# A feed-forward stage on one core: f as three 256-column products a tile, its relu taken from PSUM by ScalarE, and squares and forms issued last in a step

## The chip, the cores and the metric

The kernel runs on one NeuronCore of a Trainium2 chip. The engines named below are TensorE (PE, with its weight loads as PEld), VectorE (DVE), ScalarE (ACT), GpSimd (POOL) and SyncE (SP, which issues DMAs). The metric is the device time of one execution in microseconds (us). Before the change three runs gave 1714.46, 1715.00 and 1715.11 us, median 1715.0; the execution that was profiled took 1715.43 us, of which the span from the first to the last instruction is 1713.6 us.

## The reference, cut to what matters

One encoder block on x of 256 tokens and 2048 channels: a gated linear attention branch and a Hyena branch, merged, projected, normalized, and then the feed-forward part, which is all that the change touches:

```python
h = _layernorm(DEEPNORM_ALPHA * h + mix, ln1_g[l], ln1_b[l])
ff = jnp.square(jax.nn.relu(h @ w_ff1[l])) @ w_ff2[l]
h = _layernorm(DEEPNORM_ALPHA * h + ff, ln2_g[l], ln2_b[l])
```

`w_ff1` is 2048 x 8192 and `w_ff2` is 8192 x 2048, all float32.

## The kernel before, in words

**Precision.** Every float32 operand is split into a high part (a cast by ScalarE, `CAST hi<-src`) and a low part (VectorE subtracts the high part from the source, `TENSOR_TENSOR lo<-src,hi`). A product a·b becomes three TensorE products: high·high, high·low, low·high, summed in PSUM. So each weight block costs ScalarE one pass, VectorE one pass and TensorE three products.

**f, the first matrix.** `hT` holds the normalized input, transposed, as `hT[:, kt, part, token]` for 16 blocks `kt` of 128 channels, part 0 high and part 1 low. One tile of f is 128 feed-forward channels by 256 tokens, summed over the 16 blocks. Before the change `channel_products` makes it in one PSUM tile of 512 columns, in two halves `[:, 0]` and `[:, 1]`: per block one product of 512 columns with the high weights against high and low activations side by side (line 197, `f<-hT,whi`), and one of 256 columns with the low weights against the high activations, added to the first half (line 201, `f<-hT,wlo`). `quad_sum` then brings the two halves together: ScalarE copies the second half to `low` (`COPY f_l<-f`) and VectorE adds the first half to it, into the f tile of a pair in SBUF (`TENSOR_TENSOR dfth_fr<-f,f_l`, or `dftl_fr` or `sum_fr`: five buffers that pairs n = 0 to 31 use in turn). Two tiles (c = 0 and 1) make a pair n; `squares(n)` runs relu and then square over the pair on ScalarE (lines 1252 and 1253).

**The second matrix.** For most of `w_ff2` it is done by pairs of tiles, in Strassen-like form with seven products w0 to w6 instead of eight. `forms(n)` builds the stationary operands of a pair: three small VectorE sums (`fw`), two ScalarE casts and two VectorE subtractions into a slot of `fa`. The weights of a step arrive in a ring tile, from which `plain_split` (`b_h`, `b_l`, the two `ring` additions and two accumulating DMAs that POOL issues), `pair_split` (`whi`, `wlo` from `ring`) and `last_split` (two pieces at the end of `fa`) make the pieces. `form_products` issues three products of 512 columns for each w.

**The step.** `ff_pairs` runs 56 joint steps s = 0 to 55. Step s makes one tile of f for a later pair (n, c = divmod(s + 8, 2)) and the seven products of one pair of the second matrix. TensorE gets, in the order of the program: w0 to w2 and w3, w4 of step s, then f (both weight halves), then w5 and w6 of the step before. Meanwhile ScalarE and VectorE split what step s + 1 needs: `plain_split`, `half_split(s + 1, 0)` (the first half of f's weights, `whi`, `wlo` from `fraw`), `pair_split`, then in even steps `squares`, in the 27 steps that the table FORMED lists (5, 6, 8, 9, 10, 14, 15, 17, 19, 20 and so on) `forms`, then `quad_sum` of this step's f, then `half_split(s + 1, 1)` and `last_split`. w0 to w6 are seven PSUM banks that are summed over a run of steps (seven runs, RUNS); at a run's end `take_sums` drains them. w2, w3 and w4 hold three of the four banks of the pool that f uses, so f has one bank: the next tile of f cannot begin before this one has been drained.

**The order.** Inside `ff_pairs` the ScalarE and VectorE work, and the first and third product of each w, are pinned to the order of the program (`pin`); a scheduler places the rest, among it the products of f. Each engine runs its instructions in the order given. An engine that waits for one instruction holds up all that stand behind it.

Of the kernel before, what the change touches and what calls it, by code (L numbers as in the profile page):

```python
# [12 lines left out]
AF = mybir.ActivationFunctionType  # L13
# [3 lines left out]
P = 128  # L17
D = 2048
L = 256
NT = L // P  # L20
KT = D // P
# [10 lines left out]
LEAD = 8  # L32
# [3 lines left out]
FORMED = dict(zip((5, 6, 8, 9, 10, 14, 15, 17, 19, 20, 24, 25, 27, 29, 30, 34, 35, 37, 39, 40, 44, 45, 47, 49, 50, 53, 54,  # L36
                   SLOTS + 1), range(LEAD // 2, D_FF // P // 2)))
# [12 lines left out]
def block_kernel(  # L50
# [25 lines left out]
    nc = tc.nc  # L76
    MM = nc.tensor.matmul
# [19 lines left out]
    def psum_main(name):  # L97
        return mmp.tile([P, 512], F32, tag="mm", name=name)
# [83 lines left out]
    def channel_psum(name):  # L182
        return psum_main(name).rearrange("p (a b) -> p a b", a=2)

    def in_turn(w):
        return w.rearrange("p (a b) -> p b a", a=2)

    def both_in_turn(t):
        return t.rearrange("p k (a b) -> p k b a", a=2)

    def channel_products(ps, act, half, kts, plain=False):
        hi, lo = half
        at = [(kt, slice(kt % 8 * P, (kt % 8 + 1) * P)) for kt in kts]

        def high():
            for kt, js in at:
                MM(ps, hi[:, js], act[:, kt] if plain else both_in_turn(act[:, kt]), start=(kt == 0), stop=(kt == KT - 1))  # L197

        def low():
            for kt, js in at:  # L200
                MM(ps[:, 0], lo[:, js], act[:, kt, 0] if plain else in_turn(act[:, kt, 0]), start=False, stop=False)  # L201

        for part in (high, low) if kts[0] == 0 else (low, high):
            part()

    def channel_sum(dst, ps, name, scale=1.0):
        low = base.tile([P, L], F32, tag="low", name=name)
        with tc.high_priority():
            nc.scalar.activation(low, ps[:, 1], AF.Copy, scale=scale)
            nc.vector.scalar_tensor_tensor(dst, ps[:, 0], scale, low, op0=ALU.mult, op1=ALU.add)  # L210
# [67 lines left out]
    def act_tile(pool, tag, name):  # L278
        return pool.tile([P, KT, 2, L], F32R, tag=tag, name=name)
# [14 lines left out]
    with tc.tile_pool(name="xp", bufs=1) as xp, tc.tile_pool(name="xq", bufs=1) as xq:  # L294
# [25 lines left out]
        for i in range(3):  # L320
            t = weight_half(-1, i, True)
# [17 lines left out]
        for k0, n in PIECES:  # L339
            raw = pieces[k0]  # L340
            kts = range(k0, k0 + n)
            split_hi_lo(xT[:, k0:k0 + n, 0], xT[:, k0:k0 + n, 1], raw[:, :, 0:L])
            w = raw[:, :, L:].rearrange("p k (b j) -> p k b j", b=OPENING)
# [9 lines left out]
            if k0 == 0:  # L353
                hi, lo = places[0]
# [162 lines left out]
    for i in range(2 * NCH):  # L517
        c, o = divmod(i, 2)
        n = 4 + (i * 21) // 15
# [597 lines left out]
    hT = act_tile(ep, "hT", "hT")  # L1117
# [107 lines left out]
    def quads(n):  # L1225
        return quad_tiles[n % 5]
# [3 lines left out]
    def pin(ins):  # L1230
        return tc.keep_in_program_order(ins) if pinned[0] else ins

    def VT(dst, a, b, op):
        return pin(nc.vector.tensor_tensor(dst, a, b, op=op))  # L1234

    def cast(hi, src):
        return pin(nc.scalar.copy(hi, src))  # L1237
# [4 lines left out]
    def quad_sum(i, c, ps, name, plain=False):  # L1242
        low = base.tile([P, L], F32, tag="low", name=name)
        dst = quads(i)[:, 2 * c:2 * c + 2][:, ::-1]
        halves = [a.rearrange("p (t j) -> p t j" if plain else "p (j t) -> p t j", j=P) for a in (ps[:, 0], low)]
        with tc.high_priority():
            cast(low, ps[:, 1])
            return VT(dst, halves[0], halves[1], ALU.add)

    def squares(n):  # L1250
        q = quads(n)
        pin(nc.scalar.activation(q, q, AF.Relu))
        return pin(nc.scalar.activation(q, q, AF.Square))


    def forms(n):
        q, slot, plain = quads(n), fa_slot(n % 8), n >= SLOTS // 2
        hi, lo = slot[:, 0], slot[:, 1]
        if plain:
            cast(hi[:, 0:4], q)  # L1260
            rest(lo[:, 0:4], q, hi[:, 0:4])
            return
        t = ep.tile([P, 3, P], F32, tag="ft", name=f"fw{n}")
        VT(t[:, 0:2], q[:, 0:1].broadcast_to([P, 2, P]), q[:, 1:3][:, ::-1], ALU.subtract)
        VT(q[:, 0], q[:, 1], t[:, 0], ALU.subtract)
        VT(t[:, 2], q[:, 3], q[:, 0], ALU.subtract)
        for part, c in ((q, slice(0, 4)), (t, slice(4, 7))):
            cast(hi[:, c], part)
            rest(lo[:, c], part, hi[:, c])
# [45 lines left out]
    def last_split(p):  # L1315
        fa_slot(4)
        hi, lo = (t[:, 7168:8192] for t in fa)
        split_units(p, 2, hi, lo, raw_units(p)[:, 1:3])
# [8 lines left out]
    half_parts = {}  # L1327
# [53 lines left out]
    def take_sums(pss, p, ks):  # L1381
        if 0 <= p < SLOTS:
            begin, end, g, pair = run_of(p)
            if p == end - 1:
                for k in ks:
                    take_sum(pair == 0, g, k, pss[k])
# [30 lines left out]
    def ff_pairs():  # L1417
        pss = [psum_side(f"w{j}") if j not in (2, 3, 4) else psum_main(f"w{j}") for j in range(7)]
        joins = []
        for s in range(SLOTS):  # L1420
            more = s + 1 < SLOTS
            n, c = divmod(s + LEAD, 2)
            pinned[0] = True
            form_products(pss, s, 0, (0, 1, 2))
            form_products(pss, s, 1, (3, 4))
            ps = channel_psum(f"f{n}_{c}")
            for h in range(2):
                channel_products(ps, hT, half_parts.pop((s, h)), range(8 * h, 8 * h + 8))
            if s:
                form_products(pss, s - 1, 2, (5, 6))  # L1430
            if s + 2 < SLOTS:
                ring_load(s + 2)
            if more:
                plain_split(s + 1)
                half_split(s + 1, 0)
            take_sums(pss, s, (0, 1, 2))
            if more:
                pair_split(s + 1)
            take_sums(pss, s, (3, 4))
            if c == 0 and s:  # L1440
                squares(n - 1)
            if s in FORMED:
                forms(FORMED[s])
            quad_sum(n, c, ps, f"f{n}_l{c}")
            if more:
                half_split(s + 1, 1)
            last_split(s)
            take_sums(pss, s - 1, (5, 6))
            if s == SLOTS - 3:
                joins = join_sums(0)  # L1450
            for _ in range(min(3, len(joins))):
                joins.pop(0)()
            pinned[0] = False
            if s == SLOTS - 2:
                stop_at[0] = nblk - 4
                fetched[0] = FF_PAIRS + 2 * SLOTS
            for _ in range(max(0, s - SLOTS + 3)):
                fetch()
        squares(31)
        return pss, joins  # L1460

    def ff_close(pss, joins):
# [80 lines left out]
    ps = psum_main("w2_33_0")  # L1543
# [38 lines left out]
    with tc.high_priority(), tc.issue_after(done.ins):  # L1582
# [3 lines left out]
        y, t, v, rs = (ep.tile([P, 1], F32, tag=f"fin{i}", name=f"fin{i}") for i in range(4))  # L1586
# [164 lines left out]
```

## Time and profile before

| what | value |
|---|---|
| median of 3 runs | 1715.0 us (1714.46 to 1715.11) |
| profiled execution, and its span | 1715.43 us, 1713.6 us |
| PE, DVE, ACT, POOL busy in the span | 99%, 85%, 61%, 11% |
| granted TensorE clock | 0.999 of full speed |
| joint steps: first product of w0 in step 0 | 1095.36 us from the span's start |
| f of step 55 begins | 1649.55 us |

Busy shares are of the whole span. "Idle before" is the time for which an engine had nothing running ahead of an instruction, with what ended it. Matmuls are pipelined: a 512-column product is shown as some 380 ns long, but the next begins some 216 ns after it, so what one costs in a row of them is read from the distance between starts, or from the chain of waits, where a group's length is that distance times its count.

### The profile page before, as it was taken

The numbers are of one execution on the slowest core, as the hardware profiler recorded it, in microseconds if no ns is written. First come the engines' busy times: TensorE is split into PE (matmuls) and PEld (weight loads), VectorE is DVE, ScalarE is ACT, GpSimd is POOL, SyncE is SP. The second block draws the span as 40 slices with busy tenths as digits, with TensorE's granted clock in tenths as the row PEclk, the third lists the DMA queues.
The fourth block names the chain that finished last, engine by engine and source line by source line (L and its number), as shares of the span: only waits on it lengthen the run. The fifth ranks groups of instructions, "written<-read, shape, count | busy, mean of one in ns | idle before, by whom it ended". The sixth has DMA issues, their size and how long they took to land.

```text
span 1713.6 us, 23597 instructions
## 1 busy us (share of the span) xinstructions
PE 1691.5 (99%) x8771; PEld 1486.1 (87%) x8771; DVE 1459.7 (85%) x1899; ACT 1041.8 (61%) x1446; POOL 186.5 (11%) x243
## 2 busy tenths in 40 slices
PE   9999999999999999999999999999999999999998
PEld 8988888888888888888888889988888888888886
DVE  6789997777698989898856668999999999999998
ACT  6588876787444444444544445676766666766653
POOL 1001111000110101011000000111211112111100
PEclk9999999999999999999999999999999999999999
DMA  9678888634797979797555774688888888888864
GB/s 337 243 261 277 295 266 266 208 143 181 267 311 233 295 238 298 236 289 258 215 198 196 281 271 176 214 260 260 282 251 253 261 257 273 253 272 253 264 217 161
DMA packets 87299, 427.13 MB, mean 249 GB/s; under 512 B 9800, under 2 KB 14296, under 8 KB 45584
## 3 DMA queue, kind: packets, MB, share of 16 engines
q1 hardware_dynamic: 47664, 336.35, 52.7%
q0 software_dynamic: 30560, 67.38, 19.1%
q10 hardware_dynamic: 8960, 21.89, 3.6%
q8 instruction: 69, 1.13, 0.3%
q14 instruction: 46, 0.38, 0.1%
HBM read 382.12 MB, written 12.06 MB: 230 GB/s over the span
## 4 chain that ended last, share of the span: by engine, by line
PE 55%; DVE 18%; ACT 6%; issue 4%; DMA 1%; POOL 0%; ACTq 0%; DVEq 0%
PE f L197 6%; ACT whi L1237 4%; PE ux L249 3%; PE ux L247 3%; PE ux L248 3%; PE g L248 3%; DVE wlo L1234 3%; PE g L249 3%; PE g L247 3%; PE f L201 3%; DVE fa L1234 2%; DVE ring L1234 2%; DVE b_l L1234 2%; PE go L247 2%; PE ho L249 2%
## 5 line engine op out<-in xcount | busy, mean ns | idle before, releaser
L104 ACT CAST whi<-raw 128x1024 fp32r<-128x1024 f32 x360 | 376.1, 1050 | 360.4 <-PE ux L249 72.3
L105 DVE TENSOR_TENSOR wlo<-raw,whi 128x1024 fp32r<-128x1024 f32 x360 | 437.1, 1221 | 132.7 <-ACT whi L104 130.3
L197 PE MATMUL f<-hT,whi 128*128 128x512 f32 x984 | 234.0, 381 | 6.9 <-DVE sum_fr L1234 3.2
L197 PEld LDWEIGHTS f<-hT,whi 128*128 128x128 f32 x984 | 179.7, 189 | 36.8 <-DVE dftl_fr L1234 8.0
L1234 DVE TENSOR_TENSOR wlo<-fraw,whi 128x1024 fp32r<-128x1024 f32 x112 | 136.7, 1220 | 8.1 <-ACT whi L1237 5.7
L1237 ACT CAST whi<-ring 128x1024 fp32r<-128x1024 f32 x56 | 58.7, 1048 | 128.8 <-DVE ring L1234 91.7
L1297 POOL DMA_DIRECT2D ring<-wblk x56 | 48.6, 868 | 702.6 <-DVE ring L1234 696.2
L201 PEld LDWEIGHTS f<-hT,wlo 128*128 128x128 f32 x984 | 119.5, 192 | 3.3
L201 PE MATMUL f<-hT,wlo 128*128 128x256 f32 x984 | 119.9, 275 | 0.0
L1237 ACT CAST whi<-fraw 128x1024 fp32r<-128x1024 f32 x112 | 117.4, 1048 | 1.1 <-PE w L1379 1.1
L248 PE MATMUL g<-wlo,xT 128*128 128x512 f32 x256 | 97.6, 381 | 0.8 <-DVE wlo L105 0.8
L249 PE MATMUL ux<-whi,xT 128*128 128x512 f32 x256 | 97.3, 380 | 0.0
L248 PE MATMUL ux<-wlo,xT 128*128 128x512 f32 x256 | 97.3, 380 | 0.0
L249 PE MATMUL g<-whi,xT 128*128 128x512 f32 x256 | 97.1, 379 | 0.0
L1237 ACT CAST b_h<-ring 128x1024 fp32r<-128x1024 f32 x112 | 87.7, 832 | 10.7 <-PE w L1379 5.4
L247 PE MATMUL g<-whi,xT 128*128 128x512 f32 x256 | 89.5, 380 | 0.0
L247 PE MATMUL ux<-whi,xT 128*128 128x512 f32 x256 | 86.6, 379 | 0.0
L1234 DVE TENSOR_TENSOR ring<-ring 128x512 f32<-128x512 f32 x112 | 77.0, 688 | 1.9
L1234 DVE TENSOR_TENSOR b_l<-ring,b_h 128x1024 fp32r<-128x1024 f32 x56 | 68.3, 1219 | 3.8 <-ACT b_h L1237 3.8
L1234 DVE TENSOR_TENSOR wlo<-ring,whi 128x1024 fp32r<-128x1024 f32 x56 | 68.6, 1224 | 1.6
L1234 DVE TENSOR_TENSOR fa<-ring,fa 128x1024 fp32r<-128x1024 f32 x56 | 68.2, 1218 | 0.0
L1298 POOL DMA_DIRECT2D ring<-ring x56 | 67.2, 1200 | 0.0
(529 smaller groups left out, 4222.6 us busy)
## 6 DMA issues: line engine op xcount, KB each, us to landing
raw<-wblk SPq DMA_DIRECT2D x188, 1024.0 KB, 5.7
fraw<-wblk SPq DMA_DIRECT2D x56, 1024.0 KB, 4.9
ring<-wblk SPq DMA_DIRECT2D x56, 1024.0 KB, 7.2
ring<-wblk POOLq DMA_DIRECT2D x56, 256.0 KB, 4.6
ring<-ring POOLq DMA_DIRECT2D x56, 256.0 KB, 5.3
conv_sb<-conv_rows SPq DMA_DIRECT2D x12, 1024.0 KB, 8.7
w<-w4s ACTq DMA_DIRECT2D x16, 512.0 KB, 5.3
Td<-T POOLq DMA_DIRECT2D x32, 256.0 KB, 5.0
```

What stands on the lines that cost most here:

```text
L104: return (nc.scalar.copy(hi, src), nc.vector.tensor_tensor(lo, src, hi.bitcast(F32), op=ALU.subtract))
L105: nc.vector.tensor_tensor(lo, src, hi.bitcast(F32), op=ALU.subtract))
L197: MM(ps, hi[:, js], act[:, kt] if plain else both_in_turn(act[:, kt]), start=(kt == 0), stop=(kt == KT - 1))
L201: MM(ps[:, 0], lo[:, js], act[:, kt, 0] if plain else in_turn(act[:, kt, 0]), start=False, stop=False)
L247: order(MM(pss[tb], sh, wh, start=(kt == ends[0]), stop=False))
L248: order(MM(pss[tb], sh, wl, start=False, stop=False))
L249: order(MM(pss[tb], sl, wh, start=False, stop=(kt == ends[1])))
L1234: return pin(nc.vector.tensor_tensor(dst, a, b, op=op))
L1237: return pin(nc.scalar.copy(hi, src))
L1297: nc.gpsimd.dma_start(u[1], wblk[n, :, 1536:2048], accum_op=ALU.add)
L1298: nc.gpsimd.dma_start(u[2], u[3], accum_op=ALU.add)
```

## The change

Four things in `ff_pairs`; the first eight tiles of f (`ff1_first`) stay as they were.

1. f has one half of a PSUM bank, 256 columns. A new `channel_single` makes three products of 256 columns per block into it: high weights with high activations, high weights with low activations, low weights with high activations (line 211 of the changed kernel). The activations are read in the same interleaved order as before (`in_turn`).
2. `quad_sum` goes: no copy of a half, no VectorE sum. ScalarE's relu reads the PSUM tile and writes the f tile of the pair (line 1455, `ACTIVATE sum_fr<-f`).
3. `squares` runs the square alone.
4. `squares` and `forms` stand behind `half_split(s + 1, 1)` and `last_split(s)`, where they stood ahead of the relu's place.

```diff
+    def channel_single(ps, act, half, kts):
+        hi, lo = half
+
+        def run(w, part):
+            for kt in kts:
+                MM(ps, w[:, kt % 8 * P:(kt % 8 + 1) * P], in_turn(act[:, kt, part]), start=(kt == 0 and w is hi and part == 0),
+                   stop=(kt == KT - 1 and w is hi and part == 1))
+
+        order = ((hi, 0), (hi, 1), (lo, 0))
+        for w, part in order if kts[0] == 0 else (order[2], order[0], order[1]):
+            run(w, part)
...
-    def squares(n):
+    def squares(n, relu=True):
         q = quads(n)
-        pin(nc.scalar.activation(q, q, AF.Relu))
+        if relu:
+            pin(nc.scalar.activation(q, q, AF.Relu))
         return pin(nc.scalar.activation(q, q, AF.Square))
...
-            ps = channel_psum(f"f{n}_{c}")
+            ps = psum_main(f"f{n}_{c}")[:, 0:L]
             for h in range(2):
-                channel_products(ps, hT, half_parts.pop((s, h)), range(8 * h, 8 * h + 8))
+                channel_single(ps, hT, half_parts.pop((s, h)), range(8 * h, 8 * h + 8))
...
             take_sums(pss, s, (3, 4))
-            if c == 0 and s:
-                squares(n - 1)
-            if s in FORMED:
-                forms(FORMED[s])
-            quad_sum(n, c, ps, f"f{n}_l{c}")
+            dst = quads(n)[:, 2 * c:2 * c + 2][:, ::-1]
+            with tc.high_priority():
+                pin(nc.scalar.activation(dst, ps.rearrange("p (j t) -> p t j", t=NT), AF.Relu))
             if more:
                 half_split(s + 1, 1)
             last_split(s)
+            if c == 0 and s:
+                squares(n - 1, relu=n == LEAD // 2)
+            if s in FORMED:
+                forms(FORMED[s])
             take_sums(pss, s - 1, (5, 6))
...
-        squares(31)
+        squares(31, relu=False)
```

**How the change moves instructions.** Three places, all of them in step 10, which squares and forms pair 8 and makes the tile f9_0.

ScalarE, before. `whi207` is the pair's piece of step 11, `dftl_fr` the f tiles of pair 8 (relu, then square), `fa0` and `fw8` its forms, `f9_l0` the copied half of this step's f, `whi208_1` the second half of the next f weights:

```order
L1237 CAST whi207_0_10704<-ring2_9810 128x1024
L1252 ACTIVATE dftl_fr_9280<-dftl_fr_9280 128x512
L1253 ACTIVATE dftl_fr_9280<-dftl_fr_9280 128x512
L1237 CAST fa0_9278<-dftl_fr_9280 128x512
L1237 CAST fa0_9278<-fw8_10709 128x384
L1237 COPY f9_l0_10717<-f9_0_10649 128x256
L1237 CAST whi208_1_10721<-fraw1_9621 128x1024
L1237 CAST fa0_9278<-ring1_9683 128x1024
```

ScalarE at the same place in the changed kernel; `sum_fr` is the buffer of f9's pair:

```order
L1249 CAST whi207_0_10856<-ring2_9826 128x1024
L1455 ACTIVATE sum_fr_9281<-f9_0_10785 128x2x128
L1249 CAST whi208_1_10861<-fraw1_9621 128x1024
L1249 CAST fa0_9278<-ring1_9683 128x1024
L1266 ACTIVATE dftl_fr_9280<-dftl_fr_9280 128x512
L1249 CAST fa0_9278<-dftl_fr_9280 128x512
L1249 CAST fa0_9278<-fw8_10868 128x384
```

The instruction that reads f's bank had four instructions of pair 8 between it and the pair's cast; now it stands directly behind that cast, and the four (three now, since the relu over the pair is gone) stand behind both weight casts.

VectorE in the changed kernel, from the pair's low piece on:

```order
L1246 TENSOR_TENSOR wlo207_0_10855<-ring2_9826,whi207_0_10856 128x1024
L1246 TENSOR_TENSOR wlo208_1_10860<-fraw1_9621,whi208_1_10861 128x1024
L1246 TENSOR_TENSOR fa1_9426<-ring1_9683,fa0_9278 128x1024
L1246 TENSOR_TENSOR fw8_10868<-dftl_fr_9280 128x256
L1246 TENSOR_TENSOR dftl_fr_9280<-dftl_fr_9280,fw8_10868 128x128
L1246 TENSOR_TENSOR fw8_10868<-dftl_fr_9280 128x128
L1246 TENSOR_TENSOR fa0_9278<-dftl_fr_9280,fa0_9278 128x512
L1246 TENSOR_TENSOR fa0_9278<-fw8_10868,fa0_9278 128x384
```

Before, the five instructions of pair 8 and the sum `sum_fr<-f9_0,f9_l0` stood between the first and the second of these rows. The sum is gone, the five have moved behind the two weight pieces.

TensorE in the changed kernel, from w3 of step 10 to the end of f:

```order
L1390 MATMUL w3_9758<-whi205_0_10751,fa1_9426 128x512
L211 MATMUL f9_0_10785<-hT_8997,whi206_0_10747 128x256 x15
L1391 MATMUL w3_9758<-wlo205_0_10750,fa1_9426 128x512
L1392 MATMUL w3_9758<-whi205_0_10751,fa1_9426 128x512
L1390 MATMUL w4_9759<-whi205_0_10751,fa1_9426 128x512
L1391 MATMUL w4_9759<-wlo205_0_10750,fa1_9426 128x512
L1392 MATMUL w4_9759<-whi205_0_10751,fa1_9426 128x512
L211 MATMUL f9_0_10785<-hT_8997,whi206_0_10747 128x256
L211 MATMUL f9_0_10785<-hT_8997,wlo206_0_10746 128x256 x8
L211 MATMUL f9_0_10785<-hT_8997,wlo206_1_10755 128x256 x8
L211 MATMUL f9_0_10785<-hT_8997,whi206_1_10756 128x256 x16
```

Before, all of w3 and w4 stood ahead of f in every step. Now, in 47 of the 56 steps, up to 16 products of f (those with the first half of the high weights) stand behind w3's first product, ahead of the one that needs the low piece `wlo205`.

## The prediction

> **What bounds the kernel now.** First the page, for the engines' shares and for what the chain that ended last is made of; then the stage alone, by windows.
>
> ```profile
> span 1713.6 us, 23597 instructions
> PE 1691.5 (99%) x8771; PEld 1486.1 (87%) x8771; DVE 1459.7 (85%) x1899; ACT 1041.8 (61%) x1446; POOL 186.5 (11%) x243
> ...
> PE 55%; DVE 18%; ACT 6%; issue 4%; DMA 1%; POOL 0%; ACTq 0%; DVEq 0%
> ...
> 1107.07:1649.55 542.48, 533.72 (x2863) 471.81 (x2861) 512.57 (x646) 366.74 (x490) 94.83 (x108) 1.00 0.84 260
> 1649.55:1713.60 64.05, 55.25 (x272) 45.98 (x272) 58.82 (x95) 24.74 (x32) 1.26 (x1) 0.98 0.50 185
> ```
>
> The windows' columns are length, then busy time of PE, PEld, DVE, ACT and POOL, clock, DMA share and GB/s. The first runs from the first product of f in step 1 to the same in step 55: 54 steps, in which PE is busy for 98% and DVE for 94%. With two engines so full I ask what a step takes when nothing is late. In the timeline and the chain of waits f begins at:
>
> ```profile
> 1107.07 1.89 PE L197 MATMUL f<-hT,whi 128*128 128x512 f32 x8
> ...
> 1649.55 1.99 PE L197 MATMUL f<-hT,whi 128*128 128x512 f32 x8 [0.29 <-DVE dftl_fr L1234]
> ...
> 1117.01 1.73 PE f L197 x8
> ...
> 1126.78 1.73 PE f L197 x8
> ```
>
> An undisturbed step is 1126.78 - 1117.01 = 9.77 us of pure PE. 54 of them are 527.6 us, the stage takes 542.5: **14.9 us of PE time are lost.** Who lost them, the waits tell (total, times, longest):
>
> ```profile
> PE f L197 <- DVE sum_fr L1234: 3.2, 4, 0.8
> PE f L197 <- DVE dftl_fr L1234: 3.1, 5, 0.7
> PE w L1377 <- DVE zr L1234: 1.8, 3, 0.7
> ...
> PEld f L197 <- DVE dftl_fr L1234: 8.0, 13, 1.1
> PEld f L197 <- DVE sum_fr L1234: 4.8, 4, 1.2
> PEld f L197 <- DVE dfth_fr L1234: 1.9, 4, 0.5
> PEld w L1377 <- ACT fa L1237: 1.7, 3, 1.1
> ```
>
> The weight loads of f wait 14.7 us for exactly the VectorE sum that empties f's PSUM bank. The matmul rows give less because a matmul's modelled end overlaps the next start. w waits for drains at run ends (`zr`) and a little for `fa`: 3 us or so belong there, about 12 to f. How the sum comes to be late is seen in step 10, ScalarE first, then VectorE, then TensorE:
>
> ```profile
> 1200.79 1.05 ACT L1237 CAST whi<-ring 128x1024 fp32r<-128x1024 f32 x1 [2.19 <-PE f L197]
> 1201.74 0.63 ACT L1252 ACTIVATE dftl_fr<-dftl_fr 128x512 f32<-128x512 f32 x1
> 1202.40 0.63 ACT L1253 ACTIVATE dftl_fr<-dftl_fr 128x512 f32<-128x512 f32 x1
> 1203.91 0.62 ACT L1237 CAST fa<-dftl_fr 128x512 fp32r<-128x512 f32 x1 [0.88 <-DVE dftl_fr L1234]
> 1204.43 0.51 ACT L1237 CAST fa<-fw 128x384 fp32r<-128x384 f32 x1
> 1204.85 0.36 ACT L1237 COPY f_l<-f 128x256 f32<-128x256 f32 x1
> ...
> 1205.64 0.42 DVE L1234 TENSOR_TENSOR sum_fr<-f,f_l 128x256 f32<-128x256 f32 x1
> ...
> 1204.90 0.38 PE L1379 MATMUL w<-whi,fa 128*128 128x512 f32 x1
> 1206.12 0.70 PE L197 MATMUL f<-hT,whi 128*128 128x512 f32 x2 [0.83 <-DVE sum_fr L1234]
> ```
>
> f is complete at about 1200.76, the relu, the square and the forms of another pair go first, the sum ends at 1206.06, f starts at 1206.12. Its last w product began at 1204.90 and made room 0.22 later, at 1205.12: 1.0 us lost in this step.
>
> **The change part by part.**
>
> *TensorE: 16 products of 512 columns become 32 of 256.* The prices, from the chain (distance times count):
>
> ```profile
> 1098.76 1.73 PE f L197 x8
> 1100.48 1.78 PE f L201 x16
> 1102.27 1.73 PE f L197 x8
> ...
> 1061.34 1.88 PE f L228 x16
> 1063.70 2.85 PE f L228 x24
> ...
> L201 PE MATMUL f<-hT,wlo 128*128 128x256 f32 x984 | 119.9, 275 | 0.0
> L201 PEld LDWEIGHTS f<-hT,wlo 128*128 128x128 f32 x984 | 119.5, 192 | 3.3
> ```
>
> 512 columns: 1.73 / 8 = 0.2163 us. 256 columns: 1.78 / 16 = 0.1113. So 32 x 0.1113 - 16 x 0.2163 = 3.56 - 3.46 = +0.10 us a tile; 56 tiles, **+5.6 us**. That assumes that high weights run as the low ones of L201 do. The other bound is L228, also 256 columns, but reading the activations in plain instead of interleaved order: 2.85 / 24 = 0.119, which would make 3.80 a tile, +0.34, +19 us in all. The new products use the interleaved order of L201, so I take its price. Sixteen more weight loads a tile hide, as they do in L201, which has one for each product: 192 ns long each, and the products still start 111 ns apart.
>
> The Trainium skill's "TensorE: Matmul & The Clock Gate" (Back-to-back issue gap) gives columns / 2.4 + 2.5 ns between warm matmuls: an estimate of 109.2 and 215.8 ns, +0.04 us a tile, +2.3 us in all. The rows agree at 512 columns (216) and show 2 ns more at 256 (111), so the sum goes by the rows. The same section says that load and product set the spacing together; were the loads in the way at the 192 ns of the row, a tile would cost 32 x 0.08 = 2.6 us more and the stage 145, which L201's spacing excludes, so it gets no chance of its own.
>
> *VectorE: the sum goes; ScalarE: one relu in place of a copy and half a relu.*
>
> ```profile
> L1237 ACT COPY f_l<-f 128x256 f32<-128x256 f32 x54 | 19.6, 363 | 0.7 <-PE f L197 0.7
> L1234 DVE TENSOR_TENSOR dfth_fr<-f,f_l 128x256 f32<-128x256 f32 x22 | 10.5, 478 | 1.5 <-ACT f_l L1237 1.4
> L1252 ACT ACTIVATE dfth_fr<-dfth_fr 128x512 f32<-128x512 f32 x11 | 6.9, 625 | 0.0
> ```
>
> The relu from PSUM is not in the trace; nearest is the copy of the same 256 columns (0.36); above it is bounded by the 512-column relu (0.63). I take 0.36, and either is hidden. ScalarE gains 0.31 a step. VectorE gains 0.48 x 54 = 26 us: 512.6 - 26 = 487 us in a stage that cannot be shorter than 54 x 9.87 = 533, so its share falls from 94% to 91%.
>
> *The bank's release.* In step 10 the relu stands behind `whi<-ring`, whose successor began at 1201.74, and would end at 1202.1. The next f could use the bank 3.0 us before the old gap opened at 1205.12; and even where up to 16 products of f now stand behind w3's first product, five products earlier (1.1 us), 1.9 us are left. The cast ahead of the relu waits for VectorE's `ring` additions, so a late VectorE can still hold the relu, but only when it is some 2 us later than here. **All f waits, about 12 us, should go.**
>
> *Squares and forms last.* The same instructions, later in a step. ScalarE's next casts `b_h` and VectorE's `b_l` stand behind them now; before, the f bank and the second weight half did. What they can delay is w3's low piece, and there f's 16 first products (1.78 us) now fill in. A pair is formed two steps or more before its first use (pair 8 in step 10, for step 12), so no `fa` slot comes late.
>
> *What stays.* The waits for drains at run ends do not depend on f. I keep their 3 us and add 1 for steps in which forms now delay a piece: **4 of the 14.9 us stay.** DMAs: none added or taken, the ring load is issued behind the same `last_split`.
>
> *Behind the stage.* One sum less on VectorE, and its drains come earlier:
>
> ```profile
> 1657.46 0.46 PE L247 MATMUL w<-whi,fa 128*128 128x512 f32 x1 [1.11 <-DVE zr L1234]
> ```
>
> Of this wait I give back a third, 0.4 us (0 to 1.1).
>
> **The sum**, against the profiled execution: -14.9 + 4 + 5.6 - 0.4 = -5.7, so 1715.43 - 5.7 = 1709.7. The median of the runs shown is 0.4 below that execution: **1709.3 us**.
>
> **Rivals.**
>
> *The 256-column products run at the plain rows' pace (slower than before).* 32 x 0.119 instead of 32 x 0.1113 is 0.24 us more a tile, 13.5 in all, less some 2 us of waits that a longer step hides: 1721. For it: no row has high weights against interleaved activations at 256 columns, and none the low activations. Against: 984 products of L201 at 0.1113, and the order of reading is the only difference that the rows show. It decides from (14.9 - 4 + 0.4 + 3.46 x 56) / (56 x 32) = 0.1144 us a product.
>
> *The wait moves.* VectorE at 91% with forms at a step's end, in front of `b_l`, the ring and the pair's low piece: in consecutive steps with forms (8, 9 and 10, for instance) lateness adds up, and w waits as long as f did. If half of the 12 us return: 1715.3, no change. For it: `fa` forms wait for ScalarE in the trace and the `ring` chain is in order on both engines. Against: the sum's 0.48 us is gone from each of these steps.
>
> *Every wait goes*, run ends too, since VectorE reaches its drains earlier: 1705. For it: VectorE's gain of 26 us is more than all losses. Against: w3 and w4 end shortly before the next run needs their banks.
>
> *The relu is late all the same*, behind the forms: the order of the changed kernel excludes it.
>
> **How the numbers follow.** The forecast has 0.68, the plain pace 0.10, the moved wait 0.13, every wait gone 0.09. The range must leave out no more than 2 in 10: from 1704.0 (every wait gone, with a little of the tail) to 1715.5 (the moved wait); the plain pace stays out. The forecast's own is 1706.5 to 1712. A change of 0.2%, 3.4 us, is about what can be told from none. Faster: 0.68 + 0.09 less a little of the forecast's edge, 0.75; same: the moved wait and that edge, 0.14; slower: the plain pace and a moved wait at full, 0.11.
>
> **What would show it.** Right: f L211 in the chain at 0.111 a product; undisturbed steps of 9.87 us; no wait of f for the relu; DVE near 91% in the stage; waits of w for `zr` still there at run ends. Wrong: L211 at 0.114 or more; f waiting for ACT `sum_fr`; w L1391 waiting for `wlo`, or w for `b_h` and `b_l`, more than 4 us in total.

## The result, and the profile after

The changed kernel takes **1705.7 us** (median of 4 runs, 1705.29 to 1709.11) against 1715.0 for the kernel before in the same comparison: a ratio of **0.9946, 95% interval 0.9933 to 0.9958**, 9.3 us less. The forecast was 5.7 less, 1709.3; the time lies in its range, and the sign was right.

The page of the changed kernel's profiled execution (1705.69 us), in the order in which the page of before was read: the engines, the chain that ended last by engine, and the new products with their weight loads.

```profile
span 1703.8 us, 25339 instructions
PE 1692.4 (99%) x9667; PEld 1520.0 (89%) x9667; DVE 1440.2 (85%) x1843; ACT 1029.4 (60%) x1418; POOL 186.5 (11%) x243
...
PE 77%; DVE 4%; ACT 1%; DMA 1%; issue 1%; POOL 0%; DVEq 0%; ACTq 0%
...
L211 PE MATMUL f<-hT,whi 128*128 128x256 f32 x1792 | 222.9, 275 | 0.0
L211 PEld LDWEIGHTS f<-hT,whi 128*128 128x128 f32 x1792 | 217.4, 192 | 4.4
```

TensorE's share of the chain rose from 55% to 77%, and VectorE's fell from 18% to 4%: what ended last now hangs on TensorE's own work.

To see where the time went, the stage is cut at the first product of w5, which directly follows f in every step. In before that product of step 1 starts at 1112.31 and that of step 55 at 1654.90; in the changed kernel at 1112.65 and 1646.84. These stretches hold 54 whole steps. By windows, before first, then after (length, then busy time of PE, PEld, DVE, ACT and POOL, clock, DMA share, GB/s):

```profile
1112.31:1654.90 542.59, 533.83 (x2864) 471.92 (x2863) 512.58 (x646) 367.15 (x491) 94.42 (x108) 1.00 0.84 258
```

```profile
1112.65:1646.84 534.19, 534.19 (x3728) 503.81 (x3727) 494.95 (x593) 355.11 (x463) 93.92 (x107) 1.00 0.86 263
```

After, TensorE is busy for the whole of it: length and busy time are the same number. Nothing is lost, run ends included, and 534.19 / 54 = 9.892 us is a step of pure products. Before, an undisturbed step was 9.772 (527.7 for 54), so 14.9 us were lost. (The expectations below count 14.8 us lost and 6.4 us paid for longer steps; it is 14.9 and 6.5.)

| stretch | before | after | difference |
|---|---|---|---|
| ahead of w5 in step 1 | 1112.31 | 1112.65 | +0.34 |
| 54 steps | 542.59 | 534.19 | -8.40 = -14.9 lost + 54 x 0.120 of longer steps |
| from w5 in step 55 to the end | 58.7 | 57.0 | -1.7 |
| span | 1713.6 | 1703.8 | -9.8 |

The waits of TensorE say the same (products and weight loads, from 1090 us to the end; us in total, times, longest). Every row that named f, or w in the stage, has gone; what is left lies behind the stage and was there before too:

```profile
PE w L260 <- DVE wr L105: 1.5, 1, 1.5
PE lo L1612 <- DVE fin L1606: 1.0, 1, 1.0
...
PEld w L260 <- DVE wr L105: 2.1, 2, 1.9
```

Step 10, the one that the prediction followed, in the timeline of the changed kernel (start, length, engine; in brackets the idle time ahead and what ended it), ScalarE, VectorE, TensorE:

```profile
1202.44 1.05 ACT L1249 CAST whi<-ring 128x1024 fp32r<-128x1024 f32 x1 [1.81 <-DVE ring L1246]
1203.39 0.38 ACT L1455 ACTIVATE sum_fr<-f 128x256 f32<-128x256 f32 x1
...
1205.56 0.63 ACT L1266 ACTIVATE dftl_fr<-dftl_fr 128x512 f32<-128x512 f32 x1
1207.86 0.62 ACT L1249 CAST fa<-dftl_fr 128x512 fp32r<-128x512 f32 x1 [1.67 <-DVE dftl_fr L1246]
...
1203.51 1.23 DVE L1246 TENSOR_TENSOR wlo<-ring,whi 128x1024 fp32r<-128x1024 f32 x1
...
1205.14 1.95 PE L211 MATMUL f<-hT,whi 128*128 128x256 f32 x16
...
1207.37 0.38 PE L1391 MATMUL w<-wlo,fa 128*128 128x512 f32 x1
```

The relu empties f's bank from 1203.39 to 1203.77. The next f begins at 1205.14, 1.4 us later, with 16 products of its first high half, and w3's product with the low piece `wlo` stands behind them and four more, at 1207.37. `wlo` was ready at 1204.74. The forms still wait 1.67 us for VectorE, but now nothing of this step stands behind them except the next step's casts.

The scheduler has moved products of f further than the one place told ahead of the prediction. In the 47 steps in which they stand behind w3's first product, there are 7 to 24 of them, not up to 16. And in steps 23, 33, 43 and 52, each the first of a run, 24 products of f stand ahead of w3's first, 16 or 17 of them ahead of w0. In step 23, on TensorE and VectorE:

```profile
1321.69 1.95 PE L211 MATMUL f<-hT,whi 128*128 128x256 f32 x16
...
1323.03 1.27 DVE L1246 TENSOR_TENSOR zr<-zr,w 128x512 f32<-128x512 f32 x2
...
1325.97 0.50 PE L211 MATMUL f<-hT,wlo 128*128 128x256 f32 x3
1326.31 0.38 PE L1390 MATMUL w<-whi,fa 128*128 128x512 f32 x1
```

VectorE drains the banks of w3 and w4 until 1324.30, and w3 needs its bank only at 1326.31.

### The profile page after: what moved, and what is told of

Its sections match the earlier page's. It is cut to its first block, busy times and chain, and to the rows that moved or that the text cites. A ratio compares the mean times of both kernels' runs of the same rounds, so it can differ in the third digit from the quotient of the medians.

```text
span 1703.8 us, 25339 instructions
## 1 busy us (share of the span) xinstructions
PE 1692.4 (99%) x9667; PEld 1520.0 (89%) x9667; DVE 1440.2 (85%) x1843; ACT 1029.4 (60%) x1418; POOL 186.5 (11%) x243
## 4 chain that ended last, share of the span: by engine, by line
PE 77%; DVE 4%; ACT 1%; DMA 1%; issue 1%; POOL 0%; DVEq 0%; ACTq 0%
PE f L211 17%; PE w L1390 5%; PE w L1391 5%; PE w L1392 5%; PE ux L261 3%; PE ux L259 3%; PE ux L260 3%; PE g L260 3%; PE g L261 3%; PE g L259 3%; PE go L259 2%; PE ho L261 2%; PE go L260 2%; PE ho L259 2%; PE ho L260 2%; PE go L261 2%
## 5 line engine op out<-in xcount | busy, mean ns | idle before, releaser
L211 PE MATMUL f<-hT,whi 128*128 128x256 f32 x1792 | 222.9, 275 | 0.0
L211 PEld LDWEIGHTS f<-hT,whi 128*128 128x128 f32 x1792 | 217.4, 192 | 4.4
L1246 DVE TENSOR_TENSOR wlo<-fraw,whi 128x1024 fp32r<-128x1024 f32 x112 | 136.7, 1220 | 12.4 <-ACT whi L1249 12.3
L211 PE MATMUL f<-hT,wlo 128*128 128x256 f32 x896 | 114.0, 275 | 0.0
L211 PEld LDWEIGHTS f<-hT,wlo 128*128 128x128 f32 x896 | 109.2, 192 | 1.9
```

The costliest lines, as they stand in the source:

```text
L211: MM(ps, w[:, kt % 8 * P:(kt % 8 + 1) * P], in_turn(act[:, kt, part]), start=(kt == 0 and w is hi and part == 0), stop=(kt == KT - 1 and w ...
```

## The experiments

Two accounts of the lost 14.9 us were to be told apart. In the first (L, for load), VectorE's work is too long for TensorE's step: every step it adds f's sum, and whatever stands behind that sum or needs its result is late; relief of VectorE is the cure. In the second the order is at fault: `squares` and `forms` stand ahead of f's release, and moving them is the cure. Beside these stands the rival of the prediction on the products' pace. The lost time below is the stretch from w5 in step 1 to w5 in step 55 less 54 steps of the same kernel in which nothing waits; a step is counted from the w5 before it to its own. The products of f are placed by the scheduler, and not in the same way in every kernel: the last column counts the steps in which some of them stand between w3's first product and the one with the low piece.

| kernel | ratio to before, 95% interval | 54 steps | lost | tail | f ahead of the low piece |
|---|---|---|---|---|---|
| before | | 542.59 | 14.9 | 58.7 | 0 |
| order alone | 0.9991 (0.9980 to 1.0002) | 540.34 | 12.6 | 58.8 | 0 |
| sum alone | 0.9963 (0.9948 to 0.9978) | 534.63 | 0.4 | 58.4 | 23 |
| both: the changed kernel | 0.9946 (0.9933 to 0.9958) | 534.19 | 0.0 | 57.0 | 47 |
| relu on VectorE | 0.9970 (0.9960 to 0.9979) | 537.95 | 3.8 | 57.6 | 0 |
| plain reading | 1.0056 (1.0041 to 1.0071) | 552.59 | 0.0 | 56.8 | 47 |
| no fill-in | 0.9960 (0.9945 to 0.9975) | 536.02 | 1.8 | 57.0 | 0 |
| old f in 22 steps | 0.9956 (0.9940 to 0.9973) | 534.52 | 2.7 | 59.0 | 28 |
| old f in 14 steps | 0.9954 (0.9939 to 0.9969) | 535.82 | 3.0 | 57.0 | 36 |
| old f in 16 other steps | 0.9924 (0.9910 to 0.9937) | 532.51 | 0.0 | 57.0 | 34 |

Kernels were measured beside the kernel before in four groups, in which before itself took 1715.0, 1715.9, 1715.4 and 1716.7 us, so ratios are compared across groups and microseconds inside one.

**1. The order alone.** The kernel before, with `squares` and `forms` moved behind `last_split`; f keeps its 512 and 256 columns, the copy and VectorE's sum.

```diff
-            if c == 0 and s:
-                squares(n - 1)
-            if s in FORMED:
-                forms(FORMED[s])
             quad_sum(n, c, ps, f"f{n}_l{c}")
             if more:
                 half_split(s + 1, 1)
             last_split(s)
+            if c == 0 and s:
+                squares(n - 1)
+            if s in FORMED:
+                forms(FORMED[s])
```

> The kernel before with the order alone changed: squares and forms last in a step, f still 512 + 256 columns, still the copy of a half and VectorE's sum. Theory L (VectorE's load and the sum's place on VectorE set the loss): VectorE keeps 94% or more of the stage, most of the 14.8 us stay lost; the time falls by 1 to 4 us, to 1711 to 1714. Theory O (the order sets the loss: the forms stood ahead of the bank's release): nearly all of the 14.8 us go and the 6.4 us that three narrow products cost are not paid; 1701 to 1704, faster than the changed kernel.

1713.67 us against 1715.87: no difference that can be told from none. f no longer waits, yet 12.6 of the 14.9 us are still lost. The waits of TensorE in this kernel:

```profile
PE w L1378 <- DVE wlo L1234: 4.3, 8, 0.8
PE w L1377 <- DVE zr L1234: 3.4, 5, 0.8
...
PEld w L1378 <- DVE wlo L1234: 9.6, 18, 1.1
```

The wait has only changed its place: the product of w with the pair's low piece now waits for VectorE, and so do the first products of new runs. That is the mechanism of the prediction's rival "the wait moves", seen where VectorE still carries the sum, and where no product of f stands ahead of the low piece to cover it.

**2. The sum alone.** The changed kernel with `squares` and `forms` put back ahead of the relu.

```diff
             take_sums(pss, s, (3, 4))
+            if c == 0 and s:
+                squares(n - 1, relu=n == LEAD // 2)
+            if s in FORMED:
+                forms(FORMED[s])
             dst = quads(n)[:, 2 * c:2 * c + 2][:, ::-1]
...
             last_split(s)
-            if c == 0 and s:
-                squares(n - 1, relu=n == LEAD // 2)
-            if s in FORMED:
-                forms(FORMED[s])
```

> The changed kernel with squares and forms put back ahead of the relu. Theory L: VectorE has been relieved, the relu may come some 4 us late in steps with forms, the bank is still free in time in most; within 2 us of the changed kernel, 1706 to 1708. Theory O: f waits for the relu in steps with forms as it waited for the sum, so the 6.4 us for narrow products are paid and little is won: 1715 to 1720.

1708.43 against 1715.87. The old order costs the stage 0.44 us in this kernel, nearly all in one step:

```profile
PEld f L211 <- ACT sum_fr L1459: 0.7, 2, 0.5
```

So the sum's move alone, with the longer step that it brings, takes 14.4 of the 14.9 us away, the order alone 2.3; in length of the 54 steps that is 7.96 and 2.25 us of the 8.40. What the order still brings on top (0.9963 to 0.9946, whose intervals overlap) is 0.4 in the stage and 1.4 behind it: with the old order another product of the tail waits 1.21 us for a late low piece of `wr`. How the order inside the stage comes to set that one was not followed up.

**3. The relu on VectorE.** The changed kernel, with the relu from PSUM as one VectorE instruction instead of ScalarE's.

```diff
-                pin(nc.scalar.activation(dst, ps.rearrange("p (j t) -> p t j", t=NT), AF.Relu))
+                pin(nc.vector.tensor_scalar(dst, ps.rearrange("p (j t) -> p t j", t=NT), 0.0, None, op0=ALU.max))
```

> The changed kernel with the relu from PSUM on VectorE instead of ScalarE, at the same place: VectorE has its 0.4 us a step back. Theory L: some waits return, 1707 to 1711. Theory O: the bank is released in time all the same, 1705 to 1706.

1709.83 against 1715.87. Columns and bank are those of the changed kernel, and VectorE has 15.1 us more to do in the stretch (510.07 against 494.95). But the scheduler has also left all products of f behind w4, as in experiment 5, so the 3.8 us that are lost again are not all VectorE's. Over 1 us of them is lost in step 12, the rest mainly in steps 23, 33, 43 and 52, the first of new runs (0.72, 0.72, 0.73 and 0.32):

```profile
PE w L1390 <- DVE zr L1246: 1.4, 3, 0.5
...
PE w L1391 <- DVE wlo L1246: 0.8, 1, 0.8
...
PEld w L1391 <- DVE wlo L1246: 1.8, 5, 1.1
```

The waits for `zr` at run ends are back. How much of them is VectorE's load, experiment 5 tells.

**4. Plain reading.** The changed kernel, with the activations read in plain order, as in the products of L228 from which the slow rival had its price (the relu's view of the tile is turned to match).

```diff
-                MM(ps, w[:, ...], in_turn(act[:, kt, part]), ...)
+                MM(ps, w[:, ...], act[:, kt, part], ...)
```

> The changed kernel with the activations of f read in plain order instead of the interleaved one. The price of the 24 plain products in the trace of before, 0.119 us, against 0.1116 measured in the changed kernel's chain makes a tile 48 x 0.0074 = 0.36 us longer, 20 us in all: 1725, and slower than before. If those 24 were slow for another reason (half-tile work at the stage's start), nothing changes: 1706.

1724.91 against 1715.87, slower. The chain of waits of this kernel, and then that of the changed one (start, length, what):

```profile
1610.74 4.61 PE f L211 x39
```

```profile
1632.98 4.13 PE f L211 x37
```

4.61 / 39 = 0.1182 us a product in plain order, 4.13 / 37 = 0.1116 in interleaved order, with the same weights and the same number of columns. A step is 552.59 / 54 = 10.233 instead of 9.892 us, which is 0.0071 a product for 48 of them. Over the 32 products with high weights that is 0.23 us a tile, the rival's 0.24; the other 16, which read interleaved before too, pay it here as well. The interleaved order is the only thing that keeps the changed kernel from this price.

**5. No fill-in.** The changed kernel with the products of f pinned to the order of the program, so that none stands between w3's first product and the one with the low piece.

```diff
-                MM(ps, w[:, ...], in_turn(act[:, kt, part]), ...)
+                tc.keep_in_program_order(MM(ps, w[:, ...], in_turn(act[:, kt, part]), ...))
```

> The changed kernel with f's products pinned to the order of the program, so that none of them stands between w3's first product and the one that needs the low piece. In the changed kernel's trace of step 10 that piece ends at 1204.74; w3's second product would then stand at about 1205.1, a margin of 0.4 us, and less in the next step. Theory L (what is near the limit is now the pair's low piece, and the 1.8 us of f in front of it are its cover): w waits for wlo in steps with forms and at run ends, 1 to 5 us come back, 1707 to 1711. If there is slack enough without it: 1705 to 1706.

1708.22 against 1715.37. In the stage 1.8 us are lost, in steps 12, 23, 33, 43 and 52 (and 0.07 in step 37):

```profile
PEld w L1391 <- ACT sum_fr L1267: 1.3, 3, 0.4
PEld w L1392 <- DVE wlo L1247: 0.9, 2, 0.7
```

The first of these rows belongs to the run starts 23, 33 and 43. It names ScalarE's square, but in step 23 that was over at 1325.49, and what ran on was VectorE's drain of w3's bank, the first of the two here:

```profile
1324.87 0.62 ACT L1267 ACTIVATE sum_fr<-sum_fr 128x512 f32<-128x512 f32 x1
...
1325.00 1.28 DVE L1247 TENSOR_TENSOR zr<-zr,w 128x512 f32<-128x512 f32 x2
...
1325.80 0.19 PEld L1391 LDWEIGHTS w<-whi,fa 128*128 128x128 f32 x1 [0.43 <-ACT sum_fr L1267]
```

So the products of f placed among w's cover two things that VectorE still owes: the low piece in steps 12 and 37 (0.56 and 0.07 us), and the drains at the run starts 23, 33 and 43 (0.30 each). Step 52 loses 0.32, for which the trace names no engine. Without this cover the changed kernel would keep 13 of the 14.9 us.

As in experiment 3 all products of f stand behind w4, so these two kernels show what the relu costs on VectorE instead of ScalarE: with VectorE busy for 510.07 us instead of 494.82 the 54 steps take 537.95 instead of 536.02, 1.9 us more, and the run starts 23, 33 and 43 lose 0.72 instead of 0.30. The drains do depend on what VectorE does for f, which the prediction had denied. From before to the changed kernel there is then a chain of kernels: the order takes 2.25 us off the 54 steps (kernel 1), three narrow products with the relu on VectorE take 2.39 (kernel 3, though VectorE is as busy as in kernel 1, 510.07 against 510.75, and TensorE's own work is 6.5 longer), the move of the relu to ScalarE 1.93 (kernel 5), and f's products among w's 1.83. Another sequence would divide the 8.40 otherwise: kernel 2, with the old order, lacks only 0.44 of it.

**6. Two products in place of three.** This kernel leaves out the products of the high weights with the low activations, a third of f's work, so its time is not that of the same computation. It shortens TensorE's step to see what the other engines need.

```diff
-        order = ((hi, 0), (hi, 1), (lo, 0))
+        order = ((hi, 0), (lo, 0))
```

> The changed kernel without f's products of the high weights with the low activations (left out of the computation: 16 of 48 a tile), which takes 16 x 0.1116 = 1.79 us of TensorE from each step: 8.11 us. It shows how far VectorE is from setting the step. Theory L: VectorE, 92.7% of 9.89 busy, cannot go below some 9.2 to 9.4 us on the mean, so steps fall to about 9.3 and the whole to about 1675; w waits for wlo and b_l. If TensorE alone sets the step: 8.1 us a step and 1606.

1692.49 us (one run). 16 products less are 16 x 0.1116 = 1.79 us a step, but only 14.5 us are gained in 54 steps, 0.27 each. The windows and the waits of TensorE:

```profile
1110.28:1629.99 519.71, 460.49 (x2865) 403.36 (x2863) 494.34 (x592) 349.18 (x463) 95.04 (x108) 1.00 0.88 271
```

```profile
PE w L1390 <- ACT whi L1249: 29.9, 31, 1.1
PE w L1391 <- DVE b_l L1246: 18.8, 25, 0.8
```

519.71 / 54 = 9.62 us is the most that ScalarE and VectorE, which wait for each other, can need for a mean step, with VectorE busy for 95% of it. Without VectorE's waits for `b_h` (9.0 us in all), behind some of which stands TensorE, it would be 9.46: the need lies between these two. The steps that come two behind one with forms take 10.4 to 10.7 us (step 52, also the first of a run, 12.4); half of the others take 8.1, as long as TensorE's products alone. I had expected 9.3; the mean lies only 0.27 us below the changed kernel's 9.89. Before the change VectorE had (512.58 - 494.95) / 54 = 0.33 us more to do in a step: 9.79 to 9.95, an estimate, against TensorE's 9.77. By this estimate VectorE's mean step was as long as TensorE's or longer before, and is shorter after. The mean would account for 1 to 10 of the 14.9 us; that the rest comes of the unevenness from step to step is argued, not shown.

**7 and 8. The old f in some steps.** If the changed f is needed only where VectorE is loaded, the cheaper old products (0.120 us a step) should serve elsewhere. Both kernels keep the new order of the step.

```diff
+            wide = s not in FORMED and all(s != r[1] - 1 for r in RUNS)
-            ps = psum_main(f"f{n}_{c}")[:, 0:L]
+            ps = channel_psum(f"f{n}_{c}") if wide else psum_main(f"f{n}_{c}")[:, 0:L]
...
-                channel_single(ps, hT, half_parts.pop((s, h)), range(8 * h, 8 * h + 8))
+                (channel_products if wide else channel_single)(ps, hT, half_parts.pop((s, h)), range(8 * h, 8 * h + 8))
...
+            if wide:
+                quad_sum(n, c, ps, f"f{n}_l{c}")
```

That is kernel 7, with 22 such steps: those without forms that are not the last of a run. (`squares` runs relu and square there where a pair has such a tile.) Kernel 8 names 14:

```diff
-            wide = s not in FORMED and all(s != r[1] - 1 for r in RUNS)
+            wide = s in (0, 1, 2, 4, 7, 11, 13, 16, 23, 26, 33, 36, 43, 46)
```

> A mixture: f in 512 + 256 columns with the copy and VectorE's sum in the 22 steps that neither make forms nor end a run, three narrow products and ScalarE's relu in the other 34; squares and forms last. Theory L: 22 x 0.12 = 2.6 us of TensorE are won, VectorE gets 22 x 0.42 = 9 us back (95% of the stage), and the lateness that this leaves around steps 8 to 12, 20 to 22 and so on costs 1 to 4 us: 1703 to 1707. If VectorE's slack is the same in every step: 1703.

> The same mixture with the old f only in the 14 of these steps that lie away from run ends and rows of forms (0, 1, 2, 4, 7, 11, 13, 16, 23, 26, 33, 36, 43, 46). Theory L: 14 x 0.12 = 1.7 us won, few waits: 1704 to 1705. If any VectorE sum costs as much as it saves: 1706.

1708.03 and 1707.43 against 1715.37: neither can be told from the changed kernel. Both lose some 3 us in the same four places, steps 12, 27, 37 and 47. Kernel 8 at the first of them:

```profile
1215.22 0.48 PE L1391 MATMUL w<-wlo,fa 128*128 128x512 f32 x1 [0.40 <-DVE wlo L1246]
1215.54 0.38 PE L1392 MATMUL w<-whi,fa 128*128 128x512 f32 x1
1215.76 0.38 PE L1390 MATMUL w<-whi,fa 128*128 128x512 f32 x1
```

Each stands right behind a step with the old f (11, 26, 36, 46) that itself follows two or three steps in a row with forms. The reading was that VectorE has not caught up there, and that one more sum is enough. It does not hold as it stands. Steps 7 and 16 follow two such steps as well, and steps 8 and 17 wait in neither kernel. And on VectorE the sum of step 11 stands behind the low piece that is waited for (kernel 8):

```profile
1213.94 1.23 DVE L1246 TENSOR_TENSOR wlo<-ring,whi 128x1024 fp32r<-128x1024 f32 x1
1215.08 0.42 DVE L1246 TENSOR_TENSOR sum_fr<-f,f_l 128x256 f32<-128x256 f32 x1
```

It stands so in all eight cases, four steps in two kernels. What is missing there is the cover of experiment 5: in steps 12, 27, 37 and 47 the changed kernel has 24, 23, 23 and 23 products of f ahead of the one that needs the low piece, kernels 7 and 8 none. Behind a step with the old f no step of kernels 7 to 9 has any in that place, as one would expect of a bank that only the late sum sets free. The lack alone is not the whole cause: kernel 5 has this cover nowhere, and it loses 0.56 us in step 12, 0.07 in step 37 and nothing in 27 and 47. What adds to it there (sums of earlier steps, or TensorE's shorter steps) no run separates.

**9. The old f in 16 other steps.** Kernel 7's 22 without those four, and without 48 and 52 near the end.

```diff
+            wide = s in (0, 1, 2, 4, 7, 13, 16, 18, 21, 23, 28, 31, 33, 38, 41, 43)
```

> The changed kernel, with the old f (512 and 256 columns, the copy and VectorE's sum) in 16 steps that have neither forms nor a run's end, and that do not stand just ahead of one of the four steps that waited before: 0, 1, 2, 4, 7, 13, 16, 18, 21, 23, 28, 31, 33, 38, 41, 43. If VectorE's load right there made the four waits, none comes back: 16 x 0.12 = 1.9 us less than the changed kernel, about 1703.8. If the old f costs a wait wherever it stands, the losses are 2 to 3 us again and the time is 1706 to 1708. Shown by waits of w for wlo in the steps right after those of the list.

**1703.81 us** (5 runs, 1702.92 to 1705.18), beside the changed kernel, run again in the same group, at 1705.67 (5 runs, 1704.55 to 1707.32). The difference of the two means is 1.9 us, with a 95% interval of 0.6 to 3.2 (worked out from the ten times), a ratio of 0.9989. No wait came back, and TensorE is busy throughout:

```profile
1113.77:1646.28 532.51, 532.51 (x3504) 496.39 (x3503) 500.34 (x609) 362.12 (x479) 94.43 (x108) 1.00 0.86 264
```

14 of the 16 steps lie in this stretch: 14 x 0.120 = 1.68, the length that is missing from 534.19. This version beats both kernels. In the four steps that had waited, 24 products of f stand ahead of the low piece again; so the run shows which steps to spare, and not that VectorE's load there made the waits.

**10 to 12. The wait behind the stage.** In the changed kernel one product waits 1.45 us for `wr`, because VectorE makes the last two low pieces of `wr` behind four statistics and a sum. Kernel 10 puts them ahead; kernel 11 does so in kernel 9; kernel 12 is the changed kernel again.

```diff
     parts += resident_pieces(late_parts[:1], keep)
+    parts += resident_pieces(late_parts[1:], keep)
     for tb in range(NT):
         add_ff(second[tb], tb, 512, 512, order=keep, summed=True)
-    parts += resident_pieces(late_parts[1:], keep)
```

> The changed kernel with one difference, behind the stage: VectorE makes the last low pieces of wr ahead of the four statistics and the sum of the last f tiles of the block, not behind them. In the changed kernel a product waits 1.45 us there for wr at 1679.87. If this wait is on the path that sets the end it goes, about 1704.3; if the statistics are what sets the end (the cast of whiz then comes some 2.3 us later), the gain is lost at the next product that needs them, 1705.7 or up to 1 us more.

> Both: the 16 steps with the old f, and the other order behind the stage. If both hold, 1.9 + 1.4 = 3.3 us less than the changed kernel, about 1702.4; if either falls, that part stays away.

> The changed kernel once more, beside these three, so that they can be compared on one chip: 0.9946 of the kernel before, within 0.001; no wait of TensorE in the stage; a last wait of about 1.45 us for wr behind it.

1706.58, 1704.05 and 1705.67 us: nothing is gained. The wait for `wr` is gone from kernel 10's products, and another has grown by as much (its waits of TensorE behind the stage):

```profile
PE lo L1612 <- DVE fin L1606: 2.4, 1, 2.4
```

It was 1.0 in the changed kernel. What ends last there is VectorE's chain to `fin`, and TensorE, which waited for `wr`, had that time to spare. Kernel 12 had the same 54 steps as the first profile of this kernel to the hundredth, 534.19, while the stretch ahead of them was 1.56 us longer (w5 of step 1 at 1114.21 against 1112.65): differences of 1 to 2 us between spans lie outside the stage.

## Why the prediction was right in sign and 3.6 us short

**TensorE's products: +0.10 a tile, mis-sized a little.** Measured 9.892 - 9.772 = 0.120 a step, 6.7 us for 56 instead of 5.6. About half of the difference is the fourth decimal: 0.1116 a product in the chain (4.13 / 37), 0.1113 in L201's. The 192 ns loads hide, as forecast. The Trainium skill's "TensorE: Matmul & The Clock Gate" (Back-to-back issue gap), weighed in the prediction, makes an estimate of 109.2 ns for 256 columns; the measured 111.6 is 2.4 ns above it, and its +2.3 us in all was a third of what was paid.

**The f waits go: right.** No row of f is left, with 1.4 us to spare in step 10 (the prediction had worked out 1.9).

**"The waits for drains at run ends do not depend on f": wrong, and the largest error.** I kept 3 us of them and added 1. None stayed, for two reasons. A drain stands in VectorE's queue, so the 0.33 us of a step that VectorE no longer spends bring it forward: the run starts 23, 33 and 43 lose 0.84 us each with the order alone (experiment 1), 0.72 with the relu on VectorE (3) and 0.30 with it on ScalarE (5). The last 0.30 is gone because the scheduler put 24 products of f ahead of w3 there, which I had not seen: I counted on f's products only for the low piece. The rival "every wait goes", 1705 us, with 0.09, was the case that came. Its argument, that VectorE reaches its drains earlier, is half of the cause; the objection to it, that w3 and w4 end shortly before the next run needs their banks, was right, and f's products answer it. So part of the gain beyond the forecast was luck: nothing in my working led to it.

**VectorE from 94% to 91%: the mechanism right, the gain mis-sized.** The share is 494.95 / 534.19 = 92.7%. I took 0.48 us for each sum, 26 in all; busy time fell by 17.6, or 0.33 a step. The instructions overlap: in experiment 3 a VectorE relu is 0.42 us long, and the next instruction starts 0.34 after it began:

```profile
1205.27 0.42 DVE L1455 TENSOR_SCALAR sum_fr<-f 128x256 f32<-128x256 f32 x1
1205.61 1.22 DVE L1246 TENSOR_TENSOR wlo<-fraw,whi 128x1024 fp32r<-128x1024 f32 x1
```

The rule of the front part for matmuls, price by the distance between starts, holds for VectorE here as well. ScalarE's 0.31 a step was 0.22 ((367.15 - 355.11) / 54), probably for the same reason.

**The relu at 0.36: right** (0.38), and hidden. **Squares and forms last: the cover by f was right**, and the 1 us that I allowed for a delayed piece did not come. Experiment 1 shows that with the sum still on VectorE, and no cover, this order makes w wait for `wlo`; experiment 5 that the cover is worth 1.8 us, drains included.

**Behind the stage: 0.4 forecast, 1.7 measured.** I gave back a third of the 1.11 us that w waited for `zr`. All of it went: the first product of the next w stands 2.56 us behind w5 of step 55 in before, 1.30 after.

**The rival of the slow pace** had the right price (experiment 4) and the right condition: the order of reading decides, and the changed kernel reads interleaved.

In sum: -14.9 lost + 0 kept + 6.5 for 54 longer steps - 1.7 behind the stage + 0.3 ahead of it = -9.8 between the two spans, where the prediction had -14.9 + 4 + 5.6 - 0.4.

## What to carry to other kernels

Where two engines are both above 90% busy, compare their mean steps and not only their waits: here VectorE needed an estimated 9.8 to 9.95 us and TensorE 9.77, and reordering alone mostly moved the wait to the next instruction (12.6 of 14.9 us stayed lost). Before pricing a wait, ask what independent work could stand in front of it: a bank that is free early let the scheduler put products of f ahead of a late piece and of late drains, which was worth 1.8 us. So look at the order of every engine in each variant: an edit on one engine can also change where a scheduler puts the work of another, as in experiments 3, 7 and 8. Pay a dearer form of an operation only in steps that need it; a table by step of the lost time told which ones (16 steps gave back 1.9 us, 4 badly placed ones cost 3). A wait that the trace shows in a tail may sit on an engine with time to spare: removing 1.45 us of it gained nothing.

## What the runs showed of the hardware

**The reading order of the activations sets a narrow product's pace.** 256 columns read with alternate elements 512 bytes apart take 0.1116 us, read one after the other 0.1182 (experiment 4, 0.34 us a step). The Trainium skill's "SBUF — State Buffer" (Door 1: The DMA port swizzle, in the note on 16-byte lines) has it that accesses in one line go at full bandwidth and each new line costs; by that the plain order should be no slower. The measurement is the other way round for these products. Why, no run here shows.

**A stall costs more than the idle time that the trace gives it.** In the rows of kernel 8 above, the product after a wait of 0.40 us is shown 0.48 long instead of 0.38, and the next starts 0.32 after it, not 0.22. A product's shown end also lies 0.16 us behind the earliest start of its successor (0.38 - 0.22). So the step should lose 0.40 + 0.16 + 0.10 = 0.66 us; it lost 0.67 (10.56 against 9.89). The wait of 0.83 us behind step 10 of before agrees: 0.83 + 0.26 = 1.09, and from w5 of step 10 to w5 of step 11 it took 10.87 - 9.77 = 1.10 us longer. The 12 matmul waits that the prediction quoted (8.1 us) thus cost some 11.2; 25 of the 54 steps were longer than 9.80, so the other stalls are too short for a matmul row to show them.
